# One 512-column product for both activation parts in place of two of 256 columns

## The chip, the cores and the metric

The program runs on one core of a Trainium2 chip. The metric is the device time of one execution in microseconds; of several executions the median is taken.

## What is computed

One layer of a diffusion backbone on 256 latent tokens and 256 context tokens of 2048 features, all in float32. Both sequences are normed and modulated, go through one combined input projection `w_in`, and from its columns into two branches: a bidirectional RWKV-7 scan and a latent attention. The branches are merged by gates, projected and added to the latents; a gated feed-forward with a short convolution along the tokens follows.

```python
h_ctx = modulate(rms_norm(xc, norm_mix_pre), ch1, cs1)
out_ctx, s_ctx, kv_ctx = token_mixer(h_ctx, s0, None, None, P, emit=False)
h_lat = modulate(rms_norm(x, norm_mix_pre), sh1, sc1)
out_lat, _, _ = token_mixer(h_lat, s_ctx, ang, kv_ctx, P, emit=True)
x = x + g1 * rms_norm(out_lat, norm_mix_post)
h = modulate(rms_norm(x, norm_ffn_pre), sh2, sc2)
x = x + g2 * rms_norm(conv_ffn(h, P), norm_ffn_post)

# in token_mixer
p = h @ w_in
merged = g_rwkv * (y_rwkv @ w_rwkv_proj) + g_mla * (o @ w_mla_proj)
return merged @ w_out
# conv_ffn
u = depthwise_conv(h @ ffn_w_gate, ffn_conv_w, ffn_conv_b)
return (gelu(u) * (h @ ffn_w_val)) @ ffn_w_down
```

## The kernel before

Features lie on partitions and tokens along the free dimension, so a projection gives 128 output features (one "column", a tile of psum) at a time: its weights are the stationary operand, 128 x 128 for each of the input's k-tiles, and the activations are the moving operand, 256 tokens wide. To reach float32's precision with operands of type float32r, weights and activations are each cut into a high and a low part, and three of the four products are summed: high weights by high activations, high weights by low activations, low weights by high activations. I call these three, for one k-tile and one column, a triple.

`weights` (L148) loads up to 1024 columns of weights by one DMA on SP's queue (`raw`, L153). For each 512 of them ACT casts the high part (`whi`, L186) and DVE subtracts it from the raw weights to get the low part (`wlo`, L187); both stand in `split` (L184). Each cast takes its place in ACT's order behind the head of the block of products two blocks earlier (`HOLD`, L159). `gemm` (L163) runs the triples of four k-tiles of a block (L176, L179, L180), and after each block steps the background generators (`pump`). A scheduler then sets each engine's order from the order in which the program emits instructions, from their dependences and from its own costs.

The stages in order of time:

- `setup` and `start` (L229, L265): both sequences are normed and modulated by blocks (`hc`, `hl`: high and low part, 16 k-tiles of 256 tokens), and beside it the seven first columns of `w_in` are done for both sequences. Their psum tiles hold the context in one half and the latents in the other.
- `low_rank`, `keys`, `values_in` (L387, L405, L459): the rest of what the context needs. `wcol` (L363) gives one psum tile `g` for each column and sequence. `shift` (L372) copies it to `rp` on ACT (L379), and DVE adds neighbouring tokens (`shs`, L382).
- `branches` (L757): in the foreground the latents' other columns (receptance, values, low gate, latent attention inputs, 32 gates), then the attention: keys, queries and values from the latents (`values`, `q_rope`, `keys_queries`), 16 heads (`head`), and the attention's projection (`project_heads`, psum `pm`). In the background run the three stages of the RWKV pairs for eight pairs of heads and two halves, `stage1` to `stage3`; `stage2` inverts triangular matrices with a loop on POOL (`Z`, `Zt`, L635 and L637) and goes through scratch in HBM by several DMAs (`ti_d`, `lanes`, `TT`). A round of the background is finished before the next begins.
- `merge` (L1045): the RWKV branch's projection (`pr`) and the gates; `project` (L1063) with `w_out`: psum `o_ps`; `second_norm`, `ffn` (L1094, L1136): the feed-forward's up projections, psum `pf`, 258 columns wide (256 tokens and the shift as a column of its own); `project` with `w_down`.

A column's psum goes to its users directly. The end of a column in `project`, and of a gate's:

```python
1074            ps = self.psg.tile([128, 256], F32, tag="g", name="o_ps")
1075            self.gemm(src[i], kt, [(ps, *act)])
1076            sq = acc if i == 0 else fo.tile([128, 256], F32, tag="sq_o", name="sq_o", bufs=2)
1077            nc.scalar.activation(sq, ps, AF.Square)
1078            nc.scalar.mul(raw[:, i], ps, gg[:, i:i + 1])
1079            if i:
1080                nc.vector.tensor_tensor(acc, acc, sq, ALU.add)

482        (ps,) = self.wcol(38 + i, "l", pump)
483        g = self.sp.tile([128, 256], F32, tag="gt", name="gt")
484        nc.scalar.activation(g, ps, AF.Tanh, bias=self.gbh[:, i:i + 1], scale=0.5)
485        nc.sync.dma_start(self.gsc[i], g)
```

After the last column of a projection, PE sums `acc` over the features (`rstd`, L217), and the norm follows from it.

## Time and profile before

| | |
|---|---|
| time, median of 3 runs | 2328.25 us (2321.64, 2328.25, 2334.10) |
| profiled execution | span 2325.7 us; no other time of this execution is shown |
| PE busy | 2225.3 us, 96% |
| weight loads (PEld) | 2079.7 us, 89% |
| DVE busy | 1542.7 us, 66% |
| ACT busy | 1204.0 us, 52% |
| POOL busy | 616.6 us, 27% |
| DMA | 511.39 MB, 220 GB/s in the mean |

PE is TensorE's products, PEld its weight loads, which overlap them; DVE is VectorE, ACT ScalarE, POOL GpSimd, SP the engine whose queue issues most DMAs. L176 is line 176 of the kernel. Products overlap in PE's pipeline: each lasts longer than the distance between two starts, so busy time alone doesn't give a rate. A tile's name stands before the arrow, what is read behind it.

### The profile page before, as it was taken

The page shows a single profiled execution, that of the slowest core. Times are in us where ns is not written, and L with a number is a line of the kernel's source. Part 1 is how long each engine was busy: PE and PEld are TensorE (multiplying, and loading weights), DVE is VectorE, ACT ScalarE, POOL GpSimd, SP SyncE. Part 2 cuts the span into 40 slices and gives each one's busy share as a digit, 9 for nine tenths or more (in the row PEclk, how much of TensorE's full clock was granted, in tenths as well). Part 3 has the DMA queues.
Part 4 walks back from the last instruction along what each step waited for, and adds up shares of the span by engine and source line. Part 5 has one row for each costly group of instructions (what it writes and reads, how often), then busy time and mean ns, then how long its engine had stood idle before and what let it go on. Part 6 is the DMA issues. An engine that isn't in the chain of part 4 may idle for free.

```text
span 2325.7 us, 50524 instructions
## 1 busy us (share of the span) xinstructions
PE 2225.3 (96%) x18728; PEld 2079.7 (89%) x18728; DVE 1542.7 (66%) x2970; ACT 1204.0 (52%) x2536; POOL 616.6 (27%) x1555
## 2 busy tenths in 40 slices
PE   5999989899999999999999999979999999999996
PEld 2788989898999998888877999979999999999996
DVE  5258677766756767777767457579686868655554
ACT  3244455555555556656655335546555555554442
POOL 0100016655655655465545000011010100000000
PEclk9999999999999999999999999989999999999998
DMA  9979787767767659778566578538575757556663
GB/s 349 317 232 304 234 280 229 226 190 215 231 192 220 212 163 305 247 245 266 174 195 178 172 234 294 176 112 281 182 254 182 254 175 246 181 178 184 188 185 111
DMA packets 250454, 511.39 MB, mean 220 GB/s; under 512 B 44800, under 2 KB 104208, under 8 KB 249568
## 3 DMA queue, kind: packets, MB, share of 16 engines
q1 hardware_dynamic: 246368, 501.88, 67.7%
q0 software_dynamic: 3840, 6.30, 1.1%
q8 instruction: 147, 2.41, 0.4%
q14 instruction: 99, 0.81, 0.1%
HBM read 455.54 MB, written 52.53 MB: 218 GB/s over the span
## 4 chain that ended last, share of the span: by engine, by line
PE 64%; DMA 5%; POOL 5%; DVE 3%; issue 2%; ACT 1%; SPq 0%; DVEq 0%; POOLq 0%; ACTq 0%
PE pf L176 7%; PE pf L179 7%; PE pf L180 7%; PE o_ps L179 5%; PE o_ps L176 5%; PE o_ps L180 5%; POOL Z L637 2%; POOL Zt L635 2%; PE g L180 2%; PE g L176 2%; PE g L179 2%; PE y_ps L708 1%; PE u_ps L691 1%; DMA lanes<-ti_d 1%; PE x_ps L685 1%
## 5 line engine op out<-in xcount | busy, mean ns | idle before, releaser
L187 DVE TENSOR_TENSOR wlo<-raw,whi 128x512 fp32r<-128x512 f32 x1072 | 740.1, 697 | 368.8 <-ACT whi L186 343.3
L186 ACT CAST whi<-raw 128x512 fp32r<-128x512 f32 x1072 | 654.2, 619 | 449.0 <-PE o_ps L179 135.5
L176 PE MATMUL pf<-z,whi 128*128 128x258 f32 x1408 | 401.8, 286 | 4.6 <-ACT z L1111 4.6
L180 PE MATMUL pf<-z,wlo 128*128 128x258 f32 x1408 | 399.5, 285 | 3.2 <-DVE wlo L187 3.2
L179 PE MATMUL pf<-z,whi 128*128 128x258 f32 x1408 | 400.9, 285 | 1.2 <-DVE z L1112 1.2
L176 PE MATMUL g<-hl,whi 128*128 128x256 f32 x1120 | 330.5, 295 | 1.1 <-ACT whi L186 0.6
L180 PE MATMUL g<-hl,wlo 128*128 128x256 f32 x1120 | 326.8, 293 | 1.6 <-DVE wlo L187 1.5
L179 PE MATMUL g<-hl,whi 128*128 128x256 f32 x1120 | 323.9, 289 | 0.0
L176 PEld LDWEIGHTS pf<-z,whi 128*128 128x128 f32 x1408 | 269.0, 191 | 4.9 <-ACT z L1111 4.9
L180 PEld LDWEIGHTS pf<-z,wlo 128*128 128x128 f32 x1408 | 267.9, 191 | 3.7 <-DVE wlo L187 3.7
L179 PEld LDWEIGHTS pf<-z,whi 128*128 128x128 f32 x1408 | 269.7, 192 | 1.5 <-DVE z L1112 1.5
L635 POOL TENSOR_TENSOR Zt<-Z,lanes 128x60 f32<-128x60 f32 (+24 forms) x496 | 194.2, 392 | 131.2 <-DMA lanes<-ti_d 71.5
L180 PEld LDWEIGHTS g<-hl,wlo 128*128 128x128 f32 x1120 | 218.5, 196 | 7.4 <-DVE wlo L187 2.6
L176 PEld LDWEIGHTS g<-hl,whi 128*128 128x128 f32 x1120 | 218.9, 195 | 6.3 <-issue 2.5
L179 PEld LDWEIGHTS g<-hl,whi 128*128 128x128 f32 x1120 | 219.0, 196 | 3.1 <-issue 1.2
L338 DVE SCALAR_TENSOR_TENSOR adacc<-araw,c,adacc 128x512 f32<-128x512 f32 x240 | 181.2, 755 | 53.5 <-DMA araw<-w_ada 51.7
L637 POOL TENSOR_TENSOR Z<-Z,Zt 128x60 f32<-128x60 f32 (+24 forms) x496 | 204.3, 412 | 36.0
L179 PE MATMUL o_ps<-f,whi 128*128 128x256 f32 x704 | 198.1, 281 | 0.0
L176 PE MATMUL o_ps<-f,whi 128*128 128x256 f32 x704 | 198.1, 281 | 0.0
L180 PE MATMUL o_ps<-f,wlo 128*128 128x256 f32 x704 | 198.1, 281 | 0.0
L1090 POOL TENSOR_TENSOR raw_o<-raw_o,R_o 128x1024 f32<-128x1024 f32 x2 | 4.7, 2347 | 489.6 <-ACT R_o L1083 489.6
L179 PEld LDWEIGHTS o_ps<-f,whi 128*128 128x128 f32 x704 | 132.5, 188 | 0.0
(327 smaller groups left out, 4826.7 us busy)
## 6 DMA issues: line engine op xcount, KB each, us to landing
raw<-w_in SPq DMA_DIRECT2D x150, 512.0 KB, 5.2
araw<-w_ada SPq DMA_DIRECT2D x256, 256.0 KB, 4.7
raw<-w_fg SPq DMA_DIRECT2D x82, 512.0 KB, 3.9
raw<-w_fv SPq DMA_DIRECT2D x82, 512.0 KB, 4.2
raw<-w_down SPq DMA_DIRECT2D x80, 512.0 KB, 3.7
araw<-w_ada SPq DMA_DIRECT2D x64, 512.0 KB, 6.0
raw<-w_mla SPq DMA_DIRECT2D x32, 512.0 KB, 4.7
raw<-w_out SPq DMA_DIRECT2D x32, 512.0 KB, 4.6
```

The source lines that it names most:

```text
L176: mm = nc.tensor.matmul(ps, wh, ahi[:, k], start=k == 0 and not shared, stop=False)
L179: nc.tensor.matmul(ps, wh, alo[:, k], start=False, stop=False)
L180: nc.tensor.matmul(ps, wl, ahi[:, k], start=False, stop=k == kt - 1 and (not shared or ps is segs[-1][0]))
L186: cut = self.nc.scalar.copy(hi, src)
L187: self.nc.vector.tensor_tensor(lo, src, hi.bitcast(F32), ALU.subtract)
L338: nc.vector.scalar_tensor_tensor(acc, raw, self.c1[:, k:k + 1], acc, ALU.mult, ALU.add)
L635: nc.gpsimd.tensor_tensor(tm[:, :m, j + 1:], Z[:, :m, j:j + 1].broadcast_to([128, m, t]), N[:, j:j + 1, j + 1:].broadcast_to([128, m, t]), ...
L637: nc.gpsimd.tensor_tensor(Z[:, :m, j + 1:], Z[:, :m, j + 1:], tm[:, :m, j + 1:], ALU.subtract)
L685: nc.tensor.matmul(px[64:128, u], XS[u // 2][:, c, u % 2], st[:, u], start=True, stop=True)
L691: nc.tensor.matmul(pu[64:128, u], vu[64:128, u], xv[64:128, u], start=True, stop=True)
L708: nc.tensor.matmul(o, st[64:128, u], rt[:, d, e, c], start=False, stop=True)
L1090: mul = eng.tensor_tensor(raw[:, c], raw[:, c], R.rearrange("p (o t) -> p o t", o=1).broadcast_to([128, 4, 256]), ALU.mult)
```

## The change

Parts of one tensor that stood in two tiles now stand side by side in one: for each k-tile the activations' high part, 256 columns, and behind it the low part. The weights' two parts share a tile `wc`. The high weights then multiply both parts in one product of 512 columns into a psum tile of 512 columns, whose halves hold the two partial sums; the low weights' product adds to the first half. `take` sums the halves: ACT copies the first, DVE adds the second. The seven early columns, whose psum tile is shared by the sequences, the keys of the attention (512 columns) and the feed-forward's up projections keep three products. The core of the diff:

```diff
     def weights(self, src, n):
...
         for o in range(0, n, 512):
             pool, bufs = next(self.cuts)
-            hi = pool.tile([128, 512], F32R, tag="whi", name="whi", bufs=bufs)
-            lo = pool.tile([128, 512], F32R, tag="wlo", name="wlo", bufs=bufs)
-            cut = self.split(hi, lo, raw[:, o:o + 512])
+            w = pool.tile([128, 2, 512], F32R, tag="wc", name="wc", bufs=bufs)
+            cut = self.split(w[:, 0], w[:, 1], raw[:, o:o + 512])
             if HOLD and len(self.heads) >= HOLD:
                 self.behind(cut, self.heads[-HOLD])
-            yield hi, lo
+            yield w
     def gemm(self, src, kt, segs, pump=None, part=None, shared=False):
...
-            for i, (hi, lo) in enumerate(self.weights(src[:, k0 * 128:(k0 + kn) * 128], kn * 128)):
-                for ps, ahi, alo in segs:
+            for i, w in enumerate(self.weights(src[:, k0 * 128:(k0 + kn) * 128], kn * 128)):
+                for ps, act in segs:
                     for j in range(4):
                         k = k0 + 4 * i + j
-                        wh, wl = hi[:, j * 128:j * 128 + 128], lo[:, j * 128:j * 128 + 128]
-                        mm = nc.tensor.matmul(ps, wh, ahi[:, k], start=k == 0 and not shared, stop=False)
+                        wh, wl = w[:, 0, j * 128:j * 128 + 128], w[:, 1, j * 128:j * 128 + 128]
+                        mm = self.product(ps, wh, wl, act[:, k], k == 0 and not shared, k == kt - 1 and (not shared or ps is segs[-1][0]))
                         if j == 0:
                             head = mm
-                        nc.tensor.matmul(ps, wh, alo[:, k], start=False, stop=False)
-                        nc.tensor.matmul(ps, wl, ahi[:, k], start=False, stop=k == kt - 1 and (not shared or ps is segs[-1][0]))
                 self.heads.append(head)
                 self.pump(pump)
+    def product(self, ps, sh, sl, act, start, stop):
+        mm = self.nc.tensor.matmul
+        n = act.shape[2]
+        if ps.shape[1] == 2 * n:
+            m = mm(ps.rearrange("p (i n) -> p i n", i=2), sh, act, start=start, stop=False)
+            mm(ps[:, 0:n], sl, act[:, 0], start=False, stop=stop)
+            return m
+        m = mm(ps, sh, act[:, 0], start=start, stop=False)
+        mm(ps, sh, act[:, 1], start=False, stop=False)
+        mm(ps, sl, act[:, 0], start=False, stop=stop)
+        return m
+    def take(self, out, ps, rows=slice(0, 128)):
+        self.nc.scalar.copy(out, ps[rows, 0:256])
+        if ps.shape[1] == 512:
+            self.nc.vector.tensor_tensor(out, ps[rows, 256:512], out, ALU.add)
...
     def gate(self, i, pump):
-        nc.scalar.activation(g, ps, AF.Tanh, bias=self.gbh[:, i:i + 1], scale=0.5)
+        self.take(g, ps)
+        nc.scalar.activation(g, g, AF.Tanh, bias=self.gbh[:, i:i + 1], scale=0.5)
...
     def project(self, src, kt, act, post, g, fo, ro):
-            ps = self.psg.tile([128, 256], F32, tag="g", name="o_ps")
-            self.gemm(src[i], kt, [(ps, *act)])
+            ps = self.psg.tile([128, 512], F32, tag="g", name="o_ps")
+            self.gemm(src[i], kt, [(ps, act)])
             sq = acc if i == 0 else fo.tile([128, 256], F32, tag="sq_o", name="sq_o", bufs=2)
-            nc.scalar.activation(sq, ps, AF.Square)
-            nc.scalar.mul(raw[:, i], ps, gg[:, i:i + 1])
+            self.take(raw[:, i], ps)
+            nc.scalar.activation(sq, raw[:, i], AF.Square)
+            nc.scalar.mul(raw[:, i], raw[:, i], gg[:, i:i + 1])
```

Wherever else a column was read from psum, `take` goes first in the same way: in `shift` and `latent` it stands for ACT's copy, in `values`, `keys_queries` (queries), `project_heads` and `merge` a copy and an addition into a scratch tile go ahead of what read psum. In the whole program PE has 2912 products fewer, DVE 216 additions and ACT 144 copies more. The merge loads its input by 8 DMAs in place of 16 half as large.

The end of the last column of the down projection on PE, before (`f` are the activations' two parts, `rst_ps` and `rst_pr` the norm's products):

```order
L176 MATMUL o_ps<-f_20967,whi 128x256
L179 MATMUL o_ps<-f_20968,whi 128x256
L180 MATMUL o_ps<-f_20967,wlo 128x256
L217 MATMUL rst_ps<-const,acc_o 128x1 x2
L225 MATMUL rst_pr<-const,rst_yb 128x128 x2
```

and now:

```order
L188 MATMUL o_ps<-f,wc 128x256
L187 MATMUL o_ps<-f,wc 128x512
L188 MATMUL o_ps<-f,wc 128x256
L234 MATMUL rst_ps<-const,acc_o 128x1 x2
L242 MATMUL rst_pr<-const,rst_yb 128x128 x2
```

Three products have become two, and the norm's products stand right behind them as before.

ACT's order at the end of a column of the down projection, before:

```order
L186 CAST whi<-raw 128x512 x11
L1077 ACTIVATE sq_o<-o_ps 128x256
L1078 ACTIVATE raw_o<-o_ps,gg 128x256
L186 CAST whi<-raw 128x512 x11
L1077 ACTIVATE sq_o<-o_ps 128x256
```

and now:

```order
L203 CAST wc<-raw 128x512 x9
L197 COPY raw_o<-o_ps 128x256
L203 CAST wc<-raw 128x512
L1096 ACTIVATE sq_o<-raw_o 128x256
L203 CAST wc<-raw 128x512
L1097 ACTIVATE raw_o<-raw_o,gg 128x256
L203 CAST wc<-raw 128x512 x9
```

The copy stands where the square stood, and the square and the scaling follow with a cast of weights between each, the square behind DVE's addition.

DVE's order beside the gates, before (`wlo` the low parts of weights, `ar`, `mr`, `vs` and `bonus` steps of the RWKV stages):

```order
L593 TENSOR_TENSOR ar_8362<-ar_ps,const 128x512
L586 TENSOR_TENSOR mr<-r,G 64x4x64 x2
L699 TENSOR_TENSOR vs<-s_ps,vs 64x256
L187 TENSOR_TENSOR wlo<-raw,whi 128x512
L700 TENSOR_TENSOR vs<-vs,GC 64x256
L187 TENSOR_TENSOR wlo<-raw,whi 128x512
L593 TENSOR_TENSOR ar_8425<-ar_ps,const 128x512
L187 TENSOR_TENSOR wlo<-raw,whi 128x512 x2
L603 TENSOR_TENSOR bonus<-bo_ps,v 128x256
```

and now, at the same steps of a later pair (`gt` is the gate's tile, `g` its psum):

```order
L611 TENSOR_TENSOR ar_7294<-ar_ps,const 128x512
L604 TENSOR_TENSOR mr<-r,G 64x4x64 x2
L204 TENSOR_TENSOR wc<-raw,wc 128x512 x2
L611 TENSOR_TENSOR ar_7349<-ar_ps,const 128x512
L199 TENSOR_TENSOR gt<-g,gt 128x256
L204 TENSOR_TENSOR wc<-raw,wc 128x512
L621 TENSOR_TENSOR bonus<-bo_ps,v 128x256
L204 TENSOR_TENSOR wc<-raw,wc 128x512 x2
L717 TENSOR_TENSOR vs<-s_ps,vs 64x256
L718 TENSOR_TENSOR vs<-vs,GC 64x256
L204 TENSOR_TENSOR wc<-raw,wc 128x512 x3
L199 TENSOR_TENSOR gt<-g,gt 128x256
```

A gate's addition now stands among them, ahead of low parts of the next weights and of steps of the stages; the two kernels' orders of the background's steps differ by some places here.

## Rows read from the trace of the kernel before

**Rows 1.** The page: the span, and busy time of PE and DVE (instructions behind x).

```profile
span 2325.7 us, 50524 instructions
...
PE 2225.3 (96%) x18728; PEld 2079.7 (89%) x18728; DVE 1542.7 (66%) x2970; ACT 1204.0 (52%) x2536; POOL 616.6 (27%) x1555
```

**Rows 2.** Busy time by stretch, in the down projection; columns are in its first line.

```profile
core 0: us, PE busy (x) PEld busy (x) DVE busy (x) ACT busy (x) POOL busy (x), PEclk, DMA share, GB/s
2100.00:2200.00 100.00, 100.00 (x845) 100.00 (x844) 51.30 (x77) 48.23 (x85) 0.00 (x0) 1.00 0.63 185
```

**Rows 3.** The same by stage.

```profile
150.00:340.00 190.00, 182.99 (x1413) 172.47 (x1411) 138.82 (x248) 88.04 (x179) 14.23 (x71) 0.98 0.85 275
340.00:860.00 520.00, 503.88 (x4504) 470.61 (x4502) 363.49 (x692) 297.94 (x646) 305.24 (x737) 0.97 0.70 211
464.00:860.00 396.00, 391.98 (x3567) 362.84 (x3566) 267.18 (x517) 222.48 (x481) 226.09 (x543) 0.98 0.68 205
860.00:1105.00 245.00, 241.44 (x1993) 210.38 (x1991) 182.69 (x381) 153.33 (x360) 132.20 (x336) 0.99 0.82 261
```

**Rows 4.** Chain of waits in 464:860, 860:1105, 1280:1378, 1560:2326 us.

```profile
by line: POOL Z L637 11.0%; PE g L180 10.5%; POOL Zt L635 10.4%; PE g L176 10.4%; PE g L179 10.2%; issue 5.0%; DMA lanes<-ti_d 4.3%; DMA araw<-w_ada 2.7%; PE x_ps L685 2.4%; PE u_ps L691 2.3%; PE y_ps L708 2.1%; PE y_ps L707 1.8%; PE s_ps L
...
by line: PE v_ps L902 7.0%; PE v_ps L904 6.5%; PE v_ps L903 6.5%; PE kn_ps L176 6.5%; PE kn_ps L179 6.0%; PE kn_ps L180 6.0%; PE u_ps L691 4.0%; PE qn_ps L176 3.7%; PE y_ps L708 3.6%; PE x_ps L685 3.5%; PE s_ps L697 3.4%; PE y_ps L707 3.4%;
...
by line: PE pm L179 19.4%; PE pm L176 19.0%; PE pm L180 18.8%; DMA raw<-w_rwkv 4.8%; PE y_ps L708 4.2%; PE y_ps L707 3.8%; DMA hr_d<-hr_s 3.6%; DMA hr<-hr_d 3.5%; DMA TT<-ti_d 3.3%; DMA hr_d<-hr 3.2%; PE u_ps L691 2.5%; PE x_ps L685 1.9%; D
...
by line: PE pf L176 21.5%; PE pf L179 21.4%; PE pf L180 21.3%; PE o_ps L179 10.9%; PE o_ps L176 10.9%; PE o_ps L180 10.9%; DVE x L1091 0.5%; DVE raw_o L1090 0.5%; PE ada_ps L344 0.4%; PE rst_pr L225 0.2%; DVEq L1363 0.1%; PE rst_ps L217 0.1
```

**Rows 5.** The page: the chain over the whole span, by engine.

```profile
PE 64%; DMA 5%; POOL 5%; DVE 3%; issue 2%; ACT 1%; SPq 0%; DVEq 0%; POOLq 0%; ACTq 0%
```

**Rows 6.** Busy time by stretch, of g, then v_ps, then pm alone.

```profile
464.00:860.00 396.00, 268.43 (x1916) 244.08 (x1914) 17.93 (x40) 0.98 0.68 205
...
860.00:1105.00 245.00, 58.18 (x423) 51.76 (x421) 13.21 (x32) 17.33 (x42) 0.99 0.82 261
...
1280.00:1378.00 98.00, 81.32 (x643) 77.86 (x641) 5.47 (x13) 1.00 0.61 186
```

**Rows 7.** Timeline of PE: start us, us, engine, line, operation, names, shapes.

```profile
925.35 0.40 PE L176 MATMUL kn_ps<-ckv,whi 128*128 128x512 f32 x1
925.58 0.40 PE L179 MATMUL kn_ps<-ckv,whi 128*128 128x512 f32 x1
925.82 0.39 PE L180 MATMUL kn_ps<-ckv,wlo 128*128 128x512 f32 x1
...
928.10 0.28 PE L176 MATMUL qn_ps<-cq,whi 128*128 128x256 f32 x1
...
929.41 0.28 PE L180 MATMUL qn_ps<-cq,wlo 128*128 128x256 f32 x1
```

**Rows 8.** Groups by line on DVE and ACT: busy us, mean ns, idle before.

```profile
L187 DVE TENSOR_TENSOR stage<-v_ps,stage 128x256 fp32r<-128x256 f32 x32 | 13.2, 421 | 9.3 <-ACT stage L186 9.0
...
L379 ACT COPY rp<-g 128x256 f32<-128x256 f32 x42 | 15.3, 373 | 46.8 <-PE g L180 43.4 <-DVE shs L382 2.3 <-POOL Z L637 1.0
```

**Rows 9.** Timeline of all engines at the end of the down projection.

```profile
2306.13 0.28 PE L180 MATMUL o_ps<-f,wlo 128*128 128x256 f32 x1
...
2306.45 0.38 ACT L1077 ACTIVATE sq_o<-o_ps 128x256 f32<-128x256 f32 x1 [6.61 <-PE o_ps L180]
...
2306.86 0.43 DVE L1080 TENSOR_TENSOR acc_o<-acc_o,sq_o 128x256 f32<-128x256 f32 x1 [6.30 <-ACT sq_o L1077]
...
2307.34 0.61 PE L217 MATMUL rst_ps<-const,acc_o 128*128 128x1 f32 x4 [0.93 <-DVE acc_o L1080]
```

**Rows 10.** Groups by line on DVE: the first addition of the token shift.

```profile
L382 DVE TENSOR_TENSOR shs<-rp 128x256 f32<-128x256 f32 x26 | 11.7, 448 | 2.5 <-ACT rp L379 1.2 <-issue 0.9 <-POOL Z L637 0.2
```

**Rows 11.** Instructions of the gate's tile: duration min/median/max, first and last start.

```profile
L484 ACT ACTIVATE gt<-g,gbh x32: 468/474/477, 577.0 to 872.6; 128x256 f32<-128x256 f32 x32
...
DMA to landing us min/median/max: 1.7/2.4/6.5
```

118 lines of the change are left out of this document (56 added, 62 removed).

## The prediction

> **What bounds the kernel now.** I read the page first: a span of 2325.7 us with PE busy for 96% of it [rows 1]. PE's busy time has the tails of pipelined matmuls in it, so the rate has to come from starts. In the down projection the trace counts 845 matmuls in 100 us, 118.34 ns from one 256-column product to the next [rows 2]. DVE and ACT are busy there for about half of the time and DMA for 63%. That stretch waits for nothing but PE.
>
> Second, the same table by stage [rows 3]. The granted clock is 0.97 to 1.00 of full speed in all of them, so 2.4 GHz nearly throughout. PE is busy nearly always, also from 340 to 1105 us, where the columns of w_in and the attention's up projections alternate with the RWKV pairs' stages. DVE has 157 of 520 us and 62 of 245 us free there.
>
> Third, the chain that ended last, which shows whether a faster product ends anything sooner [rows 4, 5]. From 1560 us on it is PE nearly alone. From 464 to 860 us it is not: POOL's two lines hold 21.4%, issue 5.0%, and the three lines of the gemm (L176, L179, L180) together only 31.1% of 396 us, 123 us. The gemm issued 1916 matmuls there [rows 6], at 0.12 us about 230 us of work. So in about 53% of its time it is this work that sets the end; in the rest the kernel waits for the triangular inverse on POOL and its transfers while PE happens to be full. For the values from 860 to 1105 us the share is 20.0% of 245 us, 49 us, against 423 x 0.12 = 51 us: 97%. For the attention's projection from 1280 to 1378 us it is 57.2% of 98 us, 56 us, against 643 x 0.12 = 77 us: 73%.
>
> **The price of one triple.** A triple is now three products of 256 columns, the first two with the same weights. It becomes one of 512 and one of 256. Both spacings stand in one stretch: twelve 512-column products start from 925.35 to 928.10 us, 229.2 ns each; the eleven spacings after that, to 929.41 us, are of 256 columns, 119.1 ns each [rows 7]. So a triple goes from 3 x 119.1 = 357.3 to 229.2 + 119.1 = 348.3 ns and saves 9.0 ns. With the down projection's 118.34 ns it saves 2 x 118.34 - 229.2 = 7.5 ns. The columns streamed are the same; only the fixed part of one product falls away. I take **8 ns**, between the two, and keep 7.5 and 9.0 as ends. The weight load that is dropped saves nothing more: loads run beside the products and are in these spacings already.
>
> The Trainium skill, "TensorE: Matmul & The Clock Gate", section "Back-to-back issue gap", gives N / 2.4 + 2.5 ns at full clock, 109.2 ns for 256 columns and 215.8 for 512, so that a triple would save 2.5 ns and all of them 7 us. The rows are slower than both figures and put the fixed part at three times as much. The same section's other figure, 131 ns for each 512-column product in a real stream, would make the saving about 100 ns; the 229.2 ns measured here exclude it.
>
> **The sum.** Triples follow from the loops (16 or 44 k-tiles a column, 4 in the attention); the order of the changed kernel has just as many products fewer on PE, 2912.
> - w_in, 150 to 340 us: 22 column-and-sequence units of 16, 352 triples, 2.8 us. PE is full and little runs beside it: counted whole.
> - w_in, 340 to 870 us: 58 units, 928 triples, 7.4 us, of which 53% ends sooner: 3.9 us.
> - values and queries, 860 to 1105 us: 128 + 64 + 32 triples, 1.8 us, 97%: 1.7 us. The keys are 512 columns wide and stay.
> - attention heads: 64 triples, 0.5 us. Each head's product stands between a softmax, which is ACT's and DVE's, and the next head's scores; these and the last transfers of the inverse cover it. I count nothing, and 0.5 us is the other end.
> - attention's projection: 256 triples, 2.0 us, 73%: 1.5 us.
> - merge and w_out: 384 triples, 3.1 us; w_down: 704 triples, 5.6 us, both whole.
>
> That is 18.6 us of at most 23.3. The feed-forward's up projections (500 us) and the seven early columns have no part in it.
>
> **What it adds.** 216 DVE additions at 0.42 us (the nearest row of that shape that reads psum) and 144 ACT copies at 0.37 us [rows 8]: 91 and 53 us of engine time. In the dense stages they fit into the time that is free, half of it in w_down [rows 2]. Two places have no cover: the ends of w_out and w_down, where PE waits for the last column's norm. Now the last product starts at 2306.13, ACT's square at 2306.45, DVE's sum at 2306.86 us and PE goes on at 2307.34 [rows 9]. A copy and an addition go ahead of the square, each with its handoff as these rows have it, 0.41 + 0.48 = 0.89 us: 1.8 us for both ends. The other cost lies from 340 to 1105 us: 114 additions (48 us on DVE, which goes from 70% to 75% busy and later from 75% to 84%) and 80 copies (30 us on ACT). The chain passes through 3% of 2326 us on DVE, 70 of its 1542.7 us busy or 4.5%, and through 1% on ACT, 23 of 1204.0 us or 2% [rows 1, 5]. At those shares the new work costs 2.2 + 0.6 = 2.8 us. The bounds are nothing, since the free time would hold it, and all of it (78 us) if each lay on the chain; the row nearest is DVE's first addition of a token shift, which already stands behind ACT's copy of the same columns and sat idle for that copy only 1.2 us in 26 columns [rows 10]. The gate's tile, which has one buffer, now goes through copy, addition and activation before its store; 0.37 + 0.42 + 0.47 us and 2.4 us of transfer make about 4 us with the issue, and a gate comes every 9.5 us (32 from 577.0 to 872.6 us) [rows 11]: free.
>
> The eight DMA issues that fall away in the merge and the common tile for the weights' two parts cost nothing: the transfers keep their bytes, and the high part's next user comes one product later at most.
>
> 18.6 - 1.8 - 2.8 = **14 us** less. The span shown is the only time of the profiled execution, and the median of the runs, 2328.25 us, lies 2.6 us above it. Counted from the median: **2314 us**, 0.6% faster. What a measurement can tell from no change is about 0.5%, 11.6 us, here: 2316.6 us and below is faster, 2339.9 and above slower.
>
> **The rivals.**
> 1. *Everything passes on* (0.13). The chain's 53% is too careful, since PE is full there too: 2912 x 8 to 9 ns less 1.8 us is 21 to 24 us, 2304 to 2307 us. For it: PE's busy share of 99% from 464 to 860 us [rows 3]. Against: POOL and the transfers in that chain [rows 4].
> 2. *The branches give nothing* (0.17). The background's rounds have to be finished before the next begin, and what PE saves becomes a wait at a round's end. Left are 2.8 + 3.1 + 5.6 - 1.8 - 2.8 = 6.9 us: 2321 us, no change.
> 3. *The long product is dearer in company* (0.08). One of the first spacings, from 925.58 to 925.82 us, is 0.24 us [rows 7], as much as two of 118.34; if that holds beside 256-column products, nothing is saved and the 4.6 us are added: 2333 us, no change. The skill's 2.5 ns, above, would come out close to that side: 7 us less 4.6, 2326 us.
> 4. *Slower: DVE's queue is held by the additions* (0.12). An addition waits for ACT's copy, and that for the column's last product. Behind it on DVE stand the low parts of the next weights and the RWKV stages' steps, for which PE and POOL wait; gates never held DVE before. Each of the 114 additions between 340 and 1105 us can hold the chain for its own 0.42 us and the copy's 0.37 us; at half of that, 0.4 us, they cost 46 us instead of 2.8: 2357 us. It decides from (14 + 11.6 + 2.8) / 114 = 0.25 us an addition. For it: chains there do cross DVE, and the order shows low parts and stage steps right behind the gates' additions. Against: the token shifts' wait of 0.05 us a column [rows 10].
>
> **The numbers.** The forecast's own case has 0.50, from 2306 to 2321 us; 0.42 of that is below 2316.6 us. With rival 1, faster has 0.55. No change has 0.08 of the forecast, rivals 2 and 3, and 0.02 of rival 4: 0.35. Slower has 0.10. The range from 2298 to 2333 us leaves out most of rival 4 and little else: the low end is 9.0 ns on every triple (24 us) and the 6 us by which single runs differ from their median, the high end is rival 3.
>
> **What would show it.** In the changed profile 512-column products should start 229 ns apart and be followed by a 256-column one 118 to 119 ns later; the down projection's 704 pairs should take 5 to 6 us less, w_out and the merge 3 us less; the ends of both projections should have 0.9 us more between the last product and the ones that sum the norm. From 340 to 1105 us the time should fall by about 3 us, with waits of PE for DVE or POOL not far above today's. A gain of 8 us or more there makes rival 1 right, none makes rival 2 right, and PE waiting for low parts of weights or DVE standing before its additions for some tenths of a us each makes rival 4 right.

## The result and the profile after

The changed kernel takes 2348.45 us (median of 4 runs, 2345.53 to 2349.64), the kernel before 2327.05 us beside it: a ratio of 1.0093, 95% interval 1.0072 to 1.0114. It is 0.9% slower; the forecast was 2314 us, and 2348 lies above the range.

The page of the changed kernel, as [rows 1] and [rows 5]:

```profile
span 2346.3 us, 44820 instructions
...
PE 2214.4 (94%) x15816; PEld 1923.6 (82%) x15816; DVE 1615.6 (69%) x3186; ACT 1250.7 (53%) x2680; POOL 611.8 (26%) x1555
...
PE 60%; DMA 6%; POOL 5%; DVE 5%; ACT 3%; issue 3%; SPq 0%; DVEq 0%; POOLq 0%; ACTq 0%
```

PE has its 2912 products fewer and is busy for 11 us less, but the span is 20.6 us longer. The start times on PE at a few places say where (the last column of w_in that needs the context, the first product of the values, and so on). They are of one profiled execution of each kernel, here and in all that follows by stage, and executions of one kernel scatter: 31 of the kernel before go from 2314.56 to 2338.29 us. I therefore lean on a stage's difference only where it comes back in several kernels.

| start of | before, us | after, us | difference |
|---|---|---|---|
| last context column of w_in | 318.39 | 316.60 | -1.8 |
| first value | 881.99 | 876.27 | -5.7 |
| first scores | 1088.69 | 1108.62 | +19.9 |
| last scores | 1243.24 | 1272.62 | +29.4 |
| last of the attention's projection | 1377.61 | 1402.99 | +25.4 |
| first of the up projections | 1531.70 | 1558.64 | +26.9 |
| first of w_down | 2055.63 | 2078.56 | +22.9 |
| end | 2325.67 | 2346.30 | +20.6 |

The loss, 35 us, lies between the first value and the last scores; before and behind that the kernel gains 15 us in sum. The same stretches by engine, first before, then after (the columns are those of [rows 2]; the stretches go from one row of the table to the next):

```profile
318.39:881.99 563.60, 545.86 (x4850) 509.30 (x4848) 394.98 (x751) 326.80 (x710) 320.48 (x784) 0.98 0.71 215
881.99:1088.69 206.70, 203.31 (x1684) 177.22 (x1682) 154.29 (x320) 129.89 (x305) 106.83 (x265) 1.00 0.83 261
1088.69:1243.24 154.55, 148.53 (x1214) 122.87 (x1213) 105.78 (x279) 91.28 (x242) 77.78 (x230) 0.98 0.62 197
```

```profile
316.60:876.27 559.67, 528.72 (x3796) 446.11 (x3794) 414.72 (x807) 333.84 (x737) 307.25 (x749) 0.96 0.70 216
876.27:1108.62 232.35, 224.64 (x1606) 181.77 (x1605) 174.37 (x376) 145.08 (x353) 118.18 (x310) 0.96 0.77 239
1108.62:1272.62 164.00, 147.89 (x1137) 118.14 (x1135) 113.69 (x304) 96.05 (x251) 81.07 (x235) 0.95 0.59 185
```

From the first value to the first scores there are 224 triples, so 224 products should have gone, from 1684 to 1460. The row has 1606. Some 146 records more stand in this stretch, and they are the background's; POOL's count there goes from 265 to 310 too. Most of the background's products are plain float32 and leave two records each, as the two `rst_ps` products of the order do in [rows 9] (x4): the orders of the two programs have 72 of them more in this stretch, 498 for 426. The granted clock falls in each of the three stretches.

### The profile page after: what moved, and what is told of

Its sections match the earlier page's. It is cut to its first block, busy times and chain, and to the rows that moved or that the text cites. A ratio compares the mean times of both kernels' runs of the same rounds, so it can differ in the third digit from the quotient of the medians.

```text
span 2346.3 us, 44820 instructions
## 1 busy us (share of the span) xinstructions
PE 2214.4 (94%) x15816; PEld 1923.6 (82%) x15816; DVE 1615.6 (69%) x3186; ACT 1250.7 (53%) x2680; POOL 611.8 (26%) x1555
## 4 chain that ended last, share of the span: by engine, by line
PE 60%; DMA 6%; POOL 5%; DVE 5%; ACT 3%; issue 3%; SPq 0%; DVEq 0%; POOLq 0%; ACTq 0%
PE o_ps L187 10%; PE pf L191 7%; PE pf L190 7%; PE pf L192 7%; PE o_ps L188 5%; PE g L187 4%; POOL Z L655 2%; POOL Zt L653 2%; PE g L188 2%; PE pm L187 2%; PE pr L187 1%; PE y_ps L726 1%; PE x_ps L703 1%; DMA araw<-w_ada 1%; PE pm L188 1%
## 5 line engine op out<-in xcount | busy, mean ns | idle before, releaser
L204 DVE TENSOR_TENSOR wc<-raw,wc 128x512 fp32r<-128x512 f32 x1072 | 740.7, 698 | 353.3 <-ACT wc L203 339.4
L203 ACT CAST wc<-raw 128x512 fp32r<-128x512 f32 x1072 | 655.7, 619 | 457.5 <-PE o_ps L188 122.0
L190 PE MATMUL pf<-z,wc 128*128 128x258 f32 x1408 | 399.2, 284 | 4.6 <-ACT z L1129 4.6
L191 PE MATMUL pf<-z,wc 128*128 128x258 f32 x1408 | 400.9, 285 | 1.2 <-DVE z L1130 1.2
L192 PE MATMUL pf<-z,wc 128*128 128x258 f32 x1408 | 395.5, 282 | 3.2 <-DVE wc L204 3.2
L187 PE MATMUL g<-hl,wc 128*128 128x512 f32 x1008 | 378.5, 413 | 7.5 <-ACT wc L203 3.8
L188 PE MATMUL g<-hl,wc 128*128 128x256 f32 x1008 | 295.1, 295 | 0.4 <-DVE wc L204 0.2
L192 PEld LDWEIGHTS pf<-z,wc 128*128 128x128 f32 x1408 | 269.3, 192 | 3.4 <-DVE wc L204 3.4
L190 PEld LDWEIGHTS pf<-z,wc 128*128 128x128 f32 x1408 | 266.6, 189 | 4.9 <-ACT z L1129 4.9
L191 PEld LDWEIGHTS pf<-z,wc 128*128 128x128 f32 x1408 | 267.9, 190 | 1.5 <-DVE z L1130 1.5
L187 PE MATMUL o_ps<-f,wc 128*128 128x512 f32 x704 | 247.2, 393 | 0.0
L187 PEld LDWEIGHTS g<-hl,wc 128*128 128x128 f32 x1008 | 195.5, 195 | 52.0 <-ACT wc L203 4.2
L188 PEld LDWEIGHTS g<-hl,wc 128*128 128x128 f32 x1008 | 197.0, 195 | 5.3 <-DVE wc L204 1.2
L188 PE MATMUL o_ps<-f,wc 128*128 128x256 f32 x704 | 199.1, 283 | 0.0
L187 PEld LDWEIGHTS o_ps<-f,wc 128*128 128x128 f32 x704 | 132.2, 188 | 30.5
L188 PEld LDWEIGHTS o_ps<-f,wc 128*128 128x128 f32 x704 | 132.4, 188 | 0.0
```

Of the source, the lines that this page charges most:

```text
L187: m = mm(ps.rearrange("p (i n) -> p i n", i=2), sh, act, start=start, stop=False)
L188: mm(ps[:, 0:n], sl, act[:, 0], start=False, stop=stop)
L190: m = mm(ps, sh, act[:, 0], start=start, stop=False)
L191: mm(ps, sh, act[:, 1], start=False, stop=False)
L192: mm(ps, sl, act[:, 0], start=False, stop=stop)
L203: cut = self.nc.scalar.copy(hi, src)
```

## What the stages outside the branches show

In w_out and w_down nothing but the products sets the pace: PE is busy without a gap. Busy time of `o_ps` alone from the first product to the last, w_out and then w_down, before (PE, PEld, ACT; then clock and DMA):

```profile
1430.31:1521.33 91.02, 91.02 (x768) 91.02 (x768) 11.22 (x30) 1.00 0.59 196
2055.63:2306.13 250.50, 250.50 (x2111) 250.50 (x2112) 11.22 (x30) 1.00 0.59 174
```

and after (PE, PEld, DVE, ACT):

```profile
1457.55:1547.31 89.76, 89.76 (x511) 78.66 (x512) 6.36 (x15) 5.58 (x15) 1.00 0.61 200
2078.56:2325.62 247.06, 247.06 (x1408) 216.51 (x1408) 6.37 (x15) 5.59 (x15) 1.00 0.60 176
```

They gain 1.26 us in 256 triples and 3.44 us in 704: 4.9 ns a triple in both, not 8. The timeline of PE in the changed down projection shows how a pair runs:

```profile
2200.39 0.39 PE L187 MATMUL o_ps<-f,wc 128*128 128x512 f32 x1
2200.62 0.28 PE L188 MATMUL o_ps<-f,wc 128*128 128x256 f32 x1
2200.74 0.40 PE L187 MATMUL o_ps<-f,wc 128*128 128x512 f32 x1
```

The long product takes 0.23 us as forecast, the short one behind it 0.12. Over the whole stage the mean spacings are 230.6 and 120.5 ns, where I had 229.2 and 118.3 to 119.1 [rows 2, 7]. And the end of the stage, which answers to [rows 9]:

```profile
2325.62 0.28 PE L188 MATMUL o_ps<-f,wc 128*128 128x256 f32 x1
2325.94 0.37 ACT L197 COPY raw_o<-o_ps 128x256 f32<-128x256 f32 x1 [6.40 <-PE o_ps L188]
2326.34 0.42 DVE L199 TENSOR_TENSOR raw_o<-o_ps,raw_o 128x256 f32<-128x256 f32 x1 [6.08 <-ACT raw_o L197]
2326.80 0.42 ACT L1096 ACTIVATE sq_o<-raw_o 128x256 f32<-128x256 f32 x1 [0.49 <-DVE raw_o L199]
...
2327.82 0.58 PE L234 MATMUL rst_ps<-const,acc_o 128*128 128x1 f32 x4 [1.92 <-DVE acc_o L1099]
```

2.20 us from the last product to the norm's, before 1.21: 0.99 us for the copy and the addition, forecast 0.89.

## The experiments

Each run is timed against the kernel before on the same chip; a ratio is to it, with its 95% interval. That kernel's medians in the five comparisons are 2324.89 (e1, e2, e4, e5), 2325.48 (g1, f2, f5, f7), 2321.50 (h1, h2, e3, f4), 2326.22 (k1, k3, k6) and 2323.80 us (k4). The theories by their letters, as they came up:

- A: the evacuations' copies and additions hold the branches up.
- B: the loss is the place of the instructions in the order that the scheduler makes; any edit changes it.
- C: the joined tiles cost. D: the long products themselves bring gaps and the lower clock.
- F: a long product needs both parts of its input, and in the heads the low one comes later. G: the heads' stage only scatters.

### Parts of the change

Every place of the change can be narrow (three products, one psum of 256 columns, read as before) or wide (as changed), in this manner:

```diff
+WIDE = {...}
...
-            ps = self.psg.tile([128, 512], F32, tag="g", name="o_ps")
+            ps = self.psg.tile([128, 512 if "o" in WIDE else 256], F32, tag="g", name="o_ps")
...
-            self.take(raw[:, i], ps)
+            if "o" in WIDE:
+                self.take(raw[:, i], ps)
+                ps = raw[:, i]
```

| run | wide | median, us | ratio |
|---|---|---|---|
| e1_layout_only | nothing | 2328.80 | 1.0012 (0.9994 to 1.0030) |
| e2_take_only | all, but two products for each long one | 2332.73 | 1.0016 (0.9994 to 1.0038) |
| e4_no_attention | all but values, queries, heads | 2328.27 | 1.0010 (0.9989 to 1.0032) |
| e5_attention_only | values, queries, heads | 2331.94 | 1.0031 (1.0007 to 1.0055) |

**e1**, expected: 

> The changed kernel's joined tiles, but every product is again three of 256 columns into one psum of 256, and every column tile is read from psum as before: no 512-column product, no addition. Theory A (the evacuations' extra steps hold the branches up): 2325 to 2330 us, the same as before, scores starting within 3 us of 1088.7 us. Theory B (any edit reorders the steps that are shuffled among the branches, and an unlucky order costs tens of us): the time may land anywhere from 2315 to 2365 us, and a place where it differs from before shows the same work in another order with VectorE waiting for a load at the head of its queue. Theory C (the joined tiles themselves cost): 2350 to 2365 us, the loss of the change without its gain.

**e2** changes one thing in the changed kernel:

```diff
-            m = mm(ps.rearrange("p (i n) -> p i n", i=2), sh, act, start=start, stop=False)
+            m = mm(ps[:, 0:n], sh, act[:, 0], start=start, stop=False)
+            mm(ps[:, n:2 * n], sh, act[:, 1], start=False, stop=False)
```

Expected: 

> The changed kernel with all its two-half psums, copies and additions, but the high part's product is again two products of 256 columns, one into each half: the evacuations' cost without the gain on TensorE. 2912 triples at the 4.9 ns that w_down and w_out gained are 14 us, so where nothing else differs: 2348 + 14 = 2362 us. Theory A: 2358 to 2366 us, with the 26 us of the stage of values and queries in the same place. Theory B: the instruction order differs from the changed kernel's, so the stage from the end of w_in to the first scores may take from 206 to 240 us, and the total 2335 to 2370 us.

**e4**, expected: 

> The change everywhere but in values, queries and the heads' outputs, which keep three products of 256 columns and one psum half. Theory A: the loss of 25.6 us before the first scores and of 10 us in the heads goes, the gains stay (w_in 5, attention projection 4.5, w_out and w_down 4.7, up projections 4, less 3 at the merge and the ends): 2327 - 14 = 2313 us, 2308 to 2318. Theory B: the order is shuffled once more, 2310 to 2350 us, with the gains of w_out and w_down (4.7 us) in place whatever the branches do.

**e5**, expected: 

> The change in values, queries and the heads' outputs alone (288 triples, 1.4 us at 4.9 ns). Theory A: 2327 + 25 + 10 = 2350 to 2362 us, the loss between the end of w_in and the last head. Theory B: 2315 to 2360 us, and a loss, if there is one, may lie in w_in as well, where no product is changed.

C falls with e1. A falls with e2: all 216 additions and 144 copies are in it, and it is 0.8% below the changed kernel although every product but the keys' is short. (2332.73 us lies 2 us under B's range as well.) From the first value to the first scores it took 209.9 us. So the loss is in no part by itself, and neither half of the change adds up to it. In e4, whose code in the stage of values is that of before, this stage took 216.1 us.

### The place of the stages' products

The order on PE gives the next lead. In the programs' orders, 1040 of the background's products, nearly all of them the RWKV stages', stand ahead of the last column of w_in in the kernel before, in e1 and in e5, 1036 in e2, but 992 in the changed kernel and in e4: wherever the latents' columns of w_in have long products, the scheduler puts fewer of the stages' beside them. The run g1 makes nearly the same shift (1000) in the kernel before, without any other change:

```diff
-        col = lambda f, *args: (5.2, lambda: f(*args, 1))
+        col = lambda f, *args: (4.7, lambda: f(*args, 1))
...
-            fg += [(5.2, lambda g=g: next(g))] * 4
+            fg += [(4.7, lambda g=g: next(g))] * 4
```

**g1**, expected: 

> The kernel before, no product changed; only the weight 4.7 in place of 5.2 that a column of w_in has when the rounds of the RWKV stages are dealt out, so that 1000 products of these stages, not 1040, stand ahead of the last column, nearly as in the changed kernel (992), and 686 between there and the first scores (before 654, changed 714). Theory B, made precise (what the change costs is the place of the stages' products in the order: more of them are left to the time in which less other work stands beside them): 2335 to 2350 us, 215 to 232 us from the first value to the first scores where before has 206.7, and half-clock stretches of 115 us or more in all. Theory D (the 512-column products themselves bring the half clock): 2325 us, half-clock stretches of about 97 us as before.

Ratio 1.0072 (1.0045 to 1.0099), 2340.25 us: 0.7% slower with not one product changed, so an order alone can cost that much. The first value comes 14.5 us sooner (867.46 us). w_in's stretch, the values and the heads:

```profile
317.37:867.46 550.09, 530.82 (x4738) 495.90 (x4736) 383.90 (x732) 317.75 (x689) 308.76 (x753) 0.98 0.71 218
867.46:1088.63 221.17, 216.01 (x1779) 186.57 (x1777) 156.84 (x327) 131.02 (x307) 109.99 (x278) 0.99 0.80 248
1088.63:1257.35 168.72, 156.17 (x1211) 128.73 (x1210) 110.19 (x291) 98.63 (x260) 82.95 (x243) 0.94 0.58 184
```

95 records more than before in the stage of values, and 14.5 us more, as expected. But w_in's stretch gave up just as much, 550.09 us for 563.60: the first scores start at 1088.63 us, before at 1088.69. What the profile shows as g1's loss lies behind them, in the heads, 168.72 us for 154.55, at a granted clock of 0.94 for 0.98. So g1 shows what an order can cost, not that the values are the place. The half-clock part of the expectation missed: the mean granted clock of the execution is 0.977, which makes some 108 us at 1.2 GHz.

Three runs move the line between wide and narrow:

| run | narrow | w_in's stretch | values' stage | heads | median, us | ratio |
|---|---|---|---|---|---|---|
| f2_not_lat | latents' columns of w_in | 568.7 us | 203.1 us | 166.5 us | 2333.56 | 1.0036 (1.0017 to 1.0054) |
| f5_not_h | heads | 552.4 us | 225.6 us | 155.8 us | 2330.51 | 1.0029 (1.0009 to 1.0048) |
| f7_lat_only | all but the latents' columns | 555.0 us | 231.9 us | 153.9 us | 2335.98 | 1.0053 (1.0036 to 1.0070) |

**f2**, expected: 

> The change everywhere but in the columns of w_in that belong to the latents alone (928 of the 2912 triples, among them all gates): these keep three products. The order then has 1040 products of the stages ahead of the last column, as before, and 646 up to the first scores. Theory B: the stage from the first value to the first scores is back at 203 to 210 us and the gains of the rest remain, 352 + 224 + 64 + 256 + 384 + 704 triples less the two projection ends: 2312 to 2320 us, 0.3 to 0.5% faster than before. Theory D: half-clock stretches still grow with the 1984 long products, to 125 us or more, and the time is 2325 to 2335 us.

**f5**, expected: 

> The changed kernel but for the heads' outputs (64 triples), which keep three products. The order up to the first scores is that of the changed kernel (992 and 714). Theory B: 225 to 235 us from the first value to the first scores and 2338 to 2348 us in all, the loss of the changed kernel but for some us in the heads. Theory A in what is left of it (the heads' copy and addition in a chain of softmax and transfers cost the 20 us by which the changed kernel is above the run without the attention): 2325 to 2330 us.

**f7**, expected: 

> Only the latents' columns of w_in get the change (928 triples). The order has 984 products of the stages ahead of the last column and 722 up to the first scores, as the changed kernel. Theory B: the whole loss is here and little of the gain, 225 to 235 us from the first value to the first scores, 2340 to 2352 us in all. Theory D: a third of the long products, a third of the extra half-clock time: 2326 to 2332 us.

B is right on the stage of values in all three: 203 us with the order of before, 226 and 232 us with the changed one, whatever is long there. All eighteen kernels agree with it: the eleven with 1036 or 1040 products ahead take 203.0 to 209.9 us there, the seven with 984 to 1000 take 216.1 to 232.3. It is wrong on the totals, which lie between and miss all three of its ranges (f2's lies in D's). f2 takes more than before in w_in's stretch (563.6 us before) and in the heads (154.6), and f5, with everything long but the heads, is 0.6% below the changed kernel: its stretch of w_in is 11 us shorter than before.

### Order and products crossed

Two runs hold the order still, and so do k1, k3 and k4 below. An ordering edge from each instruction to the next on its engine, no wait with it, puts all five engines into an order taken from another kernel's program:

```diff
         Build(ctx, tc, aps).run()
+        ordered(tc, nc)
...
+    for e, s in ORDER.items():
+        at = np.cumsum(np.frombuffer(zlib.decompress(base64.b85decode(s)), dtype="<i2").astype(np.int64))
+        for a, b in zip(at, at[1:]):
+            tc.add_manual_dep(mine[e][b], mine[e][a].name, mybir.DependencyInfo(mybir.DependencyClass.NoSync, mybir.DependencyReason.DATA))
```

**h1**, expected: 

> The changed kernel, all of its products, copies and additions, but each of the five engines issues its instructions in the order that e2_take_only has (the same program with two products of 256 columns for each of 512): an ordering edge from every instruction to the next on its engine, no wait with it. Theory B (the cost of the change is the order that the scheduler makes of it): the time of e2_take_only less 2912 x 4.9 ns, 2332.7 - 14 = 2319 us, 2313 to 2325, with 205 to 212 us from the first value to the first scores. Theory D (long products bring PE gaps and the half clock whatever the order): 2333 to 2350 us, half-clock stretches of 125 us or more.

**h2**, expected: 

> The other way round: the program of e2_take_only, no 512-column product but in the keys, each engine in the order that the changed kernel has, with the two products of 256 columns side by side where that has one of 512. Theory B: the loss of the changed kernel without the products' gain, 2348 + 14 = 2362 us, 2350 to 2368, and 225 us or more from the first value to the first scores. Theory D: the time of e2_take_only, 2328 to 2337 us, half-clock stretches of about 105 us.

| | e2's order | the changed kernel's order |
|---|---|---|
| short products | e2: 1.0016 (0.9994 to 1.0038) | h2: 2349.39 us, 1.0117 (1.0103 to 1.0131) |
| long products | h1: 2334.63 us, 1.0053 (1.0027 to 1.0079) | changed kernel: 1.0093 (1.0072 to 1.0114) |

The order alone costs 1.0% with short products (h2 has none but the keys', and is as slow as the changed kernel). D falls with that: h2's granted clock is 0.971 over the whole execution without the long products, the changed kernel's 0.969. h2's time lies just under B's range and far above D's; h1's lies above B's and in D's, so something else was missing. Between the two with long ones lies 0.4%, and in e2's order the long products lose 0.4% instead of gaining 0.6%; these two intervals overlap by a little. Two rows of the waits of PE from the first scores to the last, of e2 and of h1 (engine, tile, line, released by; us in total, times, longest), say where:

```profile
PE o_ps L188 <- ACT hd L205: 1.2, 3, 0.5
PE o_ps L189 <- DVE hd L206: 1.1, 2, 0.7
```

```profile
PE o_ps L188 <- DVE hd L205: 14.2, 14, 2.7
```

`hd` are the softmax's weights in two parts, the high one cast by ACT, the low one subtracted by DVE. In e2 the first product needs the high part only, and the order has other work on PE before many of the second ones. The long product needs both at once. With the heads' products behind the last scores it is 16 waits, 15.8 us.

### The heads' products

Two runs test this. k1 is h1, with the heads' 64 long products taken apart again, at the places that e2's order has for the two; k3 is e2 in its own order, in which the heads' first product takes the low part (the second diff, against the three products of the first).

```diff
-                    self.product(po, vg[:, 0, c], vg[:, 1, c], z, kk == 0, kk == 3)
+                    mm(po[:, 0:n], vg[:, 0, c], z[:, 0], start=kk == 0, stop=False)
+                    mm(po[:, n:2 * n], vg[:, 0, c], z[:, 1], start=False, stop=False)
+                    mm(po[:, 0:n], vg[:, 1, c], z[:, 0], start=False, stop=kk == 3)
```

```diff
-                    mm(po[:, 0:n], vg[:, 0, c], z[:, 0], start=kk == 0, stop=False)
-                    mm(po[:, n:2 * n], vg[:, 0, c], z[:, 1], start=False, stop=False)
+                    mm(po[:, n:2 * n], vg[:, 0, c], z[:, 1], start=kk == 0, stop=False)
+                    mm(po[:, 0:n], vg[:, 0, c], z[:, 0], start=False, stop=False)
```

**k1**, expected: 

> h1 (the changed kernel in the order of e2), but the heads' 64 triples are three products of 256 columns again, into the same two psum halves and at the same places of the order. Theory F (a 512-column product can only start when both parts of its input are there, and in the heads the low part comes from DVE one step later): PE's 16 waits for DVE's low part before the heads' products, 15.8 us, go back to 2 or 3 us, the heads take 160 to 165 us instead of 173.5, and the total is 2334.6 - 10 = 2325 us, 2320 to 2328. Theory G (the heads' stage scatters by 10 us from kernel to kernel whatever is done): 2330 to 2340 us.

**k3**, expected: 

> e2 (no 512-column product but in the keys) in its own order, but of the heads' three products for a k-tile the one with the low part of the softmax's weights stands first, and that with the high part second: the first product now waits for DVE's low part as a 512-column product does. Nothing else differs. Theory F: PE waits some 16 times and 10 to 16 us for DVE's low part there, the heads take 168 to 175 us instead of 161.3, and the total is 2332.7 + 10 = 2343 us, 2337 to 2347. Theory G: 2328 to 2338 us, and the waits that it shows are not seen in the total.

k1: 2316.86 us, ratio 0.9973 (0.9953 to 0.9993), 0.3% faster than the kernel before, so neither the ordering edges nor 2848 long products cost by themselves. k3: 2350.69 us, ratio 1.0115 (1.0088 to 1.0143), 1.0% slower than e2 by the exchange of two products in each of 64 triples. The heads' stretch of k1, of e2 and of k3:

```profile
1087.64:1249.02 161.38, 152.00 (x1220) 125.15 (x1221) 114.45 (x305) 96.20 (x257) 88.28 (x260) 0.96 0.61 193
```

```profile
1088.36:1249.65 161.29, 152.23 (x1222) 125.25 (x1221) 114.52 (x306) 96.34 (x257) 89.55 (x260) 0.96 0.61 193
```

```profile
1079.74:1260.93 181.19, 165.07 (x1222) 135.84 (x1221) 115.19 (x306) 96.67 (x257) 87.83 (x262) 0.88 0.55 173
```

and the wait in k3, which k1 has as small as e2:

```profile
PE o_ps L1027 <- DVE hd L206: 12.5, 12, 2.7
```

The 12 waits are 12.5 us, but the stretch is 20 us longer than e2's. PE is idle there for 7 us more, and the same 1222 records keep it busy for 12.8 us more: the mean granted clock is 0.88 in place of 0.96, so PE is at 1.2 GHz for longer. h1 and k1 differ by 12.3 us in their profiled executions, 12.1 of them in the heads (173.51 and 161.38 us). So F's wait is shown where e2's order is held, in both directions; its ranges were too narrow, with k1 below 2320 and k3 above 2347 us. G does not explain these two pairs, but the scatter that it names is there: with three short products in the usual order, the heads took from 153.9 (f7) to 168.7 us (g1) in thirteen kernels. In an order of the scheduler's own the long products don't stand out from it: f2 took 166.5 us, k6 below, the same but for the heads, 166.8.

In its own order the changed kernel gives the heads' long products later places. k4 keeps that order on all engines and takes only these 64 apart, side by side.

**k4**, expected: 

> The changed kernel with each engine in its own order, but the heads' 64 long products are two of 256 columns each again, side by side at the place of the long one, into the same psum halves. If the order carries the whole loss (the scheduler has put each long product of the heads where both of its parts are ready, and everything behind it accordingly): as the changed kernel, 2344 to 2352 us, with a few waits of PE for DVE's low part there, as in the changed kernel (3 waits, 7.6 us). If the long products of the heads carry their 15 us (the difference between f5 and the changed kernel) in this order too: 2330 to 2337 us.

k4: 2339.63 us, ratio 1.0063 (1.0045 to 1.0082), between the two cases. k1 and k4 have the same instructions, all 2848 other long products and the ordering edges with them, and differ in the order alone: 0.9%. What is left to the changed kernel, 0.3%, is the heads' long products in this order; there the intervals overlap. Where the order costs is shown by w_in's stretch and the values' of k1 and then of k4:

```profile
319.27:881.61 562.34, 537.97 (x3905) 451.43 (x3903) 414.49 (x812) 336.64 (x741) 321.94 (x784) 0.97 0.70 216
881.61:1087.64 206.03, 204.85 (x1468) 166.96 (x1466) 169.83 (x365) 140.93 (x340) 103.71 (x252) 0.98 0.82 257
```

```profile
317.50:879.20 561.70, 530.57 (x3797) 447.72 (x3795) 416.27 (x806) 333.46 (x737) 312.07 (x753) 0.96 0.69 215
879.20:1105.82 226.62, 220.46 (x1607) 177.98 (x1605) 174.96 (x378) 144.69 (x353) 117.97 (x306) 0.98 0.79 245
```

108 records have left the columns of w_in, and that stretch is as long as it was: PE is busy there for 7.4 us less and idle for 6.8 us more. That the background's chain of POOL and transfers [rows 4] sets the end there fits, but is not shown, and it does not hold in every order: g1 and f5 took 550.1 and 552.4 us. 139 records have come to the values, where PE is busy for 204.85 of 206.03 us, and that stretch grows by 20.6 us, 15.6 of them busy time. That is nearly all of the 21.2 us between the two profiled executions.

The order moves waits too. In k4 and in the changed kernel, not in k1, PE waits over 6 us near 595 us for a step of stage 3 on DVE (`vs`). The rows of PE and of DVE in the changed kernel:

```profile
594.82 0.68 PE L715 MATMUL s_ps<-TT,kb 128*64 128x64 f32 x8
601.90 1.09 PE L703 MATMUL x_ps<-vs,xs 128*64 128x64 f32 x8 [6.39 <-DVE vs L718]
```

```profile
597.82 0.43 DVE L717 TENSOR_TENSOR vs<-s_ps,vs 64x256 f32<-64x256 f32 x1
598.28 0.43 DVE L570 TENSOR_TENSOR bk<-kd,Gi 128x256 f32<-128x256 f32 x1
598.62 0.42 DVE L572 TENSOR_TENSOR bk<-ta,Gi 128x256 f32<-128x256 f32 x1
598.96 0.69 DVE L552 TENSOR_TENSOR_SCAN L<-const,sg 128x260 f32<-128x260 f32 x1
599.57 0.73 DVE L355 SCALAR_TENSOR_TENSOR adacc<-araw,c,adacc 128x512 f32<-128x512 f32 x1
...
601.33 0.42 DVE L718 TENSOR_TENSOR vs<-vs,GC 64x256 f32<-64x256 f32 x1
```

Between the two halves of the step, L717 and L718, stand steps of a stage 1 and of the modulation (`adacc`). No addition of the change is among them. That this wait costs time is not shown: k1 has one of 6.4 us for POOL near 373 us, and its stretch is equally long. And the clock, before and after PE's wait:

```profile
594.00:599.00 5.00, 1.24 (x12) 0.90 (x12) 4.82 (x12) 3.20 (x9) 0.18 (x1) 0.98 0.78 193
599.00:609.00 10.00, 6.36 (x31) 5.60 (x32) 9.85 (x23) 6.19 (x15) 5.70 (x15) 0.50 0.73 206
```

PE was busy for 1.24 of 5 us, and then has 1.2 GHz for 10 us.

### Versions that leave the losers out

**e3** (wide in the merge, w_out, w_down), expected: 

> The change in the merge, w_out and w_down alone, 1088 of the 2912 triples, behind all the branches; the order of the branches is that of the kernel before. 1088 x 4.9 ns = 5.3 us less 0.95 us at each of the two projection ends: 3 us, 2320 to 2324 us beside 2325 for the kernel before, 0.1% and no difference that can be measured. w_down's products should take 3.4 us less than before and w_out's 1.3 us less, as in the changed kernel. Theories B and D agree here; a loss would make both incomplete.

**f4** (those, the attention's projection and w_in's context columns), expected: 

> The change in the columns of w_in that the context needs too, in the attention's projection, the merge, w_out and w_down: 352 + 256 + 1088 = 1696 triples, 8.3 us less 1.9 us at the two ends. The order has 1040 products of the stages ahead of the last column of w_in and 646 from there to the first scores, as the run e1. Theory B: 2316 to 2322 us, 0.2 to 0.3% faster than before. Theory D: half-clock stretches of 115 us or more, 2325 to 2332 us.

**k6** (all but the latents' columns and the heads), expected: 

> The change without the latents' columns of w_in and without the heads: 1920 of the 2912 triples, with 1040 products of the stages ahead of the last column of w_in and 646 up to the first scores, as in the run e1. Theories B and F together: 1920 x 4.9 = 9.4 us less 1.9 us at the two ends, 2314 to 2319 us beside 2323 for the kernel before, 0.3% faster. If the loss has another cause than order and heads: 2325 to 2335 us.

e3 takes 2322.37 us, a ratio of 0.9998 (0.9980 to 1.0016), f4 2319.68 us, 0.9995 (0.9976 to 1.0015), k6 2330.36 us, 1.0020 (1.0001 to 1.0039). w_down took 247.06 us in e3 and f4, as in the changed kernel, but so small a gain can't be told in the total. k6 missed. Its stage of values is right (203.6 us), but w_in's stretch took 570.0 us against 563.3 in f4, with the same products there, and the heads 166.8 against 157.3. What makes the difference wasn't tried; e1, with the same products in w_in's stretch, took 554.6 us there, so one execution of each can't tell. Of all versions only k1 is faster than both kernels beyond its interval.

## Why the prediction was wrong

- **The sign.** The step that failed is one that the sum never named: it took the branches' work to stay in its places ("PE is full and little runs beside it: counted whole", "of which 53% ends sooner"), and priced products by the stretch in which they stand now. I had the orders of both kernels, saw that the stages' steps "differ by some places", and did not count how many lie ahead of the last column of w_in. They are 48 fewer. By k1 against k4 the order costs 0.9%, 21 us, and by e2 against h2 1.0%. From 340 to 1105 us I forecast 3 us less; the first scores start 19.9 us later.
- **The 53%.** The share can't be checked by itself: w_in's stretch got 3.9 us shorter, the forecast's figure by chance, for some 120 of the background's records are gone from it. In the two pairs that differ in the order alone (k1 and k4, e2 and h2) such a loss of work shortened it by less than 1 us or not at all, and what left it was paid in the values; in g1 and f5 the stretch did get shorter, by 13.5 and 11.2 us. What decides between the two is open.
- **The heads.** "I count nothing, and 0.5 us is the other end." The mechanism was missing: not the product's length but its input. The wait for the low part costs 0.8% in e2's order, which leaves no room for it (k1 against h1), 1.0% as k3 shows it, and some 0.3%, within the intervals, in the changed kernel's own order.
- **The price.** 8 ns a triple, 4.9 measured. Both spacings were mis-sized: before, w_down's products stand 118.7 ns apart (250.50 us for 2112), now the long one takes 230.6 ns for 229.2 and the short one behind it 120.5. With 4.9 ns the sum would have been 18.6 x 4.9 / 8 = 11.4 us less 4.6, 7 us. k1, without the heads' wait and in another order than the changed kernel's, is 0.27% or 6 us faster than the kernel before, close to these 7; part of that may be the up projections' (523.9 to 520.2 us), which no product of the change explains. By the gap that the Trainium skill, "TensorE: Matmul & The Clock Gate", section "Back-to-back issue gap", states for single products, a triple would save an estimated 2.5 ns: the measured price lies about midway between that and mine.
- **The other stages.** w_in up to its last context column gained 1.8 us of 2.8. From the last scores to the last of the attention's projection 134.4 us became 130.4, 4 us where I had 1.5. w_down 3.4 us of 5.6, w_out 1.3 of 2.0, each end about 1 us where 0.89 was forecast. The merge gained nothing: from its first product to w_out's, 47.5 us before and 49.2 us after. The up projections, whose products are unchanged, took 4 us less (523.9 and 519.9 us); with joined tiles the other kernels took 519.5 to 522.1 us, e1 519.8 without any long product, and g1, with tiles as before, 522.9.
- **The additions.** 2.8 us forecast; e2 with all of them is 0.16% above the kernel before, within its interval, so they can't be told from nothing. Rival 4 had the sign, and a time 9 us off (2357 us), with the wrong mechanism. From 340 to 1110 us DVE stood idle before the additions for 21.9 us in the changed kernel, 0.19 us each, but for 29.6 us in k1, which is faster; the gates' are the largest group, in the changed kernel and in k1:

```profile
DVE gt L199 <- ACT gt L197: 11.5, 10, 2.6
```

```profile
DVE gt L200 <- ACT gt L198: 18.2, 13, 2.6
```

PE waited for an addition there only once, 3.7 us in the changed kernel.
- **Rival 2** had it that the branches give nothing, and that is not refuted. From e2 to k1 the gain is 0.43%, 10 us, of which w_down and w_out make 7.5 (253.3 to 247.1 and 91.0 to 89.8 us); the 2.5 us that are left for all else lie within the intervals.

Open is why the scheduler puts fewer steps of the stages beside long products, why w_in's stretch gives time back in some orders and not in others, and how the 0.3% of the heads and the order divide in the changed kernel beyond their intervals.

## What to carry to other kernels

Where a scheduler sets the order, an edit of the main stream moves the background too: count in the two orders how much of it stands ahead of each stage's end, and price what moved by the stage that it moves into. Work that leaves a stretch in which the engine is not the only bound may gain nothing there (k1 and k4), and costs in a stretch in which the engine is. An operation that joins two inputs starts when the later is there; where a producer delivers one step behind another, keep the operations apart and leave the later one its place.

## What was not expected of the hardware

- The 512-column products of w_down come in two spacings, 224 to 225 ns (about a third) and 233 to 235 ns, mean 230.6 ns.
- Joined tiles with short products made w_down slower, 253.31 us in e1 against 250.50 (253.3 in e2, e5, f7, h2 and k3 too, 250.50 in g1), and left w_out at 91.02 us, with the same weight tiles in both. Against e1 the long products gain 6.25 us in w_down, 8.9 ns a triple, near the forecast's price; what the joined tile costs there wasn't tried.

```profile
1426.11:1517.13 91.02, 91.02 (x768) 91.02 (x768) 11.22 (x30) 1.00 0.57 196
2046.76:2300.07 253.31, 253.31 (x2111) 253.31 (x2112) 11.24 (x30) 1.00 0.57 172
```

- A wait can cost more than its length: the exchange of two products in k3 made 12.5 us of waits and a stretch 20 us longer, in which the same products kept PE busy for 12.8 us more at a granted clock of 0.88 for 0.96.
